# A four-mixer decoder layer: matmuls placed by a clock of two engines, norm sums in float32r, buffers of the closing parts

## The chip, the cores and the metric

The kernel runs on one core of one Trainium2 chip. A core has TensorE (matmuls, from SBUF into PSUM), VectorE, ScalarE and GpSimd, and SyncE, which here only issues DMAs. The metric is the device time in microseconds, the median of several runs.

## The reference

One layer of a hybrid decoder over a prompt of 1024 positions and, beside it, 8 single-position samples with states of their own. Both go through the same weights, so the kernel treats them as 1032 columns.

```python
hn = rmsnorm(x, norm_mix_g)
proj = hn @ w_in                       # 1024 -> 2836, columns shared out among four mixers
o_s5  = s5_mixer(...)                  # complex diagonal recurrence, gelu, gate
o_ssd = ssd_mixer(...)                 # conv, scan; rmsnorm over 256 channels of y * silu(z)
o_hg  = hgrn2_mixer(...)               # gated scan; rmsnorm over 64 channels of each head, gate
o_gla = gla_mixer(...)                 # gated scan; rmsnorm over 64 channels of each head, gate
x = x + concat(o_s5, o_ssd, o_hg, o_gla) @ w_out
hn = rmsnorm(x, norm_mlp_g)
x = x + square(relu(hn @ w_up)) @ w_down      # 1024 -> 4096 -> 1024
y = rmsnorm(x, norm_final_g)           # and the final states of the four mixers
```

All is float32.

## The kernel before

Activations lie transposed, channels on the 128 partitions and positions along the columns. The columns are cut in two halves, `hf` 0 with 512 and `hf` 1 with 520 (two chunks of 260, `CK`). A large product takes its two operands split by `split` into a high and a low float32r part (ScalarE copies `hi`, VectorE subtracts to get `lo`) and adds three matmuls for each pair (`mm3`): high with high, high with low, low with high. So one output tile of 128 rows from 8 tiles of input takes 24 matmuls of 512 columns, or 48 of 260.

`main` issues the large products in this order: input projection of half 0 (`xA`), of half 1 (`xB`), output projection of half 0 (`mixA`), its MLP, output projection of half 1 (`mixB`), its MLP (in which `fast_up` forms blocks of the up product from sums and differences of blocks, `TS`), and `close`. `side` and `side2` issue the mixers of half 0 and then of half 1 as strands: Python generators that yield where the next matmul needs work of other engines. Their small products are plain float32.

`drive` merges main and strands into one order. It keeps a clock `pe` of TensorE, which `mm` advances by a planned cost; `lat` collects the planned latency of ScalarE and VectorE instructions of a strand's step, and after the step the strand is due again at `pe + wait()`. While no strand is due, main goes on by one product step. The order is a priority: the framework's scheduler then lists each engine's instructions by priority as its own model finds them ready, so an order on an engine can differ from the order of issue. Instructions under `first()` (evictions of the large products) and the weight preparation `wprep` go ahead of the rest. Each engine and each DMA queue then works through its list in order.

The places that the change touches:

- `gated` (mixers HGRN2 and GLA) and `ssd` end with a norm: ScalarE squares the outputs into `osq` or `ysq`, TensorE multiplies them by a constant matrix (`bo64`, blocks of 1/64, or `o256`, all 1/256) held in the constants `CS`, which sums over channels and spreads the sum, and ScalarE takes `Ln` and `Exp`. Then the mixer's two tiles are split into the mixed columns (`mixed`, `mix_split`) that the output projection reads. The projection takes its eight input tiles in `MIX_ORDER`, those of `ssd` (2 and 3) last.
- `outproj` needs, for each of its 8 tiles, the weights, a load of the input `x` and a PSUM bank or two of the four called `pm`. It adds the product to `x`, splits the scaled sum into `h2`, squares it into `sq` and stores it as `xd`. The first half is finished meanwhile: in `outproj(1)`, `finish(n)` for n below 8 calls `residual` (load `xr`, scale and add to `Y`) and `sumsq` (square into another `sq`, add into `fsq`).
- `x`, both `sq`, `xr`, the evictions and some more take turns in one set of four buffers, tag `io`. The mixers' pool `mp` has 13 buffers of the same size, tag `b`; the mixers use them till their end, and the pool is closed behind `outproj(1)`. The pool `late` opens in its place.
- `close` makes the last down products of half 1 in two column chunks, `c` 1 and then 0: eight tiles, each added to `Y`, squared, summed up, scaled by the gain; then the sum over channels on TensorE, the reciprocal root (`rstd`: `Ln`, `Exp` and a correcting step on VectorE), four scalings of `Y` by it and four stores.

Of the kernel before, what the change touches and what calls it, by code (L numbers as in the profile page):

```python
# [9 lines left out]
F32 = mybir.dt.float32  # L10
# [11 lines left out]
WM = 520  # L22
# [23 lines left out]
def _layout(items):  # L46
    d, o = {}, 0
    for n, w in items:
# [6 lines left out]
                     ('dsk', 2), ('sng', 2), ('lbl', 2), ('hng', 2), ('bgk', 1), ('gng', 1), ('wgk', 128)])  # L55
PS5, NPS5 = _layout([('lre', 8), ('lim', 8), ('ldt', 8), ('bglu', 2), ('Bre', 128), ('Bim', 128), ('Cre', 128),
                     ('Cim', 128), ('sd', 128), ('dsel', 16), ('iota', 128), ('wglu', 512)])
CST, NCST = _layout([('ident', 128), ('tri', 128), ('mneg', 128), ('bo64', 128), ('o256', 128),
                     ('ones', 128), ('id32', 32), ('sel2', 2), ('sel4', 4)])


def host_consts():
    c = np.zeros((128, NCST), np.float32)

    def put(n, v):
        o, w = CST[n]
        c[:, o:o + w] = v
    i = np.arange(128)
    put('ident', np.eye(128))
    put('tri', i[:, None] <= i[None, :])  # L70
    put('mneg', np.where(i[:, None] <= i[None, :], 0.0, -1e30))
    put('bo64', (i[:, None] // 64 == i[None, :] // 64) / 64.0)
    put('o256', 1.0 / 256)
    put('ones', 1.0)
    put('id32', i[:, None] % 32 == np.arange(32)[None, :])
    put('sel2', i[:, None] // 64 == np.arange(2)[None, :])
    put('sel4', i[:, None] // 32 == np.arange(4)[None, :])
    m = np.zeros((128, 5, 16), np.int32)
    j = i % 32
    for l in range(5):  # L80
        h = 1 << l
        blk = np.arange(16) // h
        m[:, l] = (j[:, None] // (2 * h) == blk[None, :]) & (j[:, None] % (2 * h) < h)
    return c, m.reshape(128, 80)
# [26 lines left out]
class Kern:  # L111
    def __init__(self, tc, ctx, I, O):
        self.tc, self.nc, self.ctx, self.I, self.O = tc, tc.nc, ctx, I, O
        self.uid = 0
        self.pe = self.lat = self.dlat = 0.0

    def first(self):
# [4 lines left out]
        self.uid += 1  # L122
        return f"{s}_{self.uid}"

    def b(self, shape, name='t'):
        pool, tag, nb = self.here[:3]
        return pool.tile([128] + list(shape), F32, tag='b' + tag, name=self.n(name), bufs=nb)

    def q8(self, shape, name='t'):
        pool, tag = self.here[:2]  # L130
        return pool.tile([128] + list(shape), F32, tag='q' + tag, name=self.n(name), bufs=2)

    def sm(self, shape, tag, dt=F32, bufs=1):
        return self.smp.tile([128] + list(shape), dt, tag=tag, name=self.n(tag), bufs=bufs)
# [20 lines left out]

    def act(self, out, in_, f=AF.Copy, **k):
        self.lat += 250 + width(out) / 1.2
        return self.nc.scalar.activation(out, in_, f, **k)  # L158

    def dve(self, out):  # L160
        self.lat += 90 + width(out) / 0.96

    def tt(self, out, a, b_, op=OP.mult):
        self.dve(out)
# [21 lines left out]
    def mm(self, out, l, r, start=True, stop=True, token=None, **k):  # L186

        n, m = width(r), width(l)
        if l.dtype == F32R:
            self.pe += n / 2.4  # L190
        elif m > 64:
            self.pe += 426 if n < 128 else 1.7 * n
        else:
            self.pe += max(80, 1.05 * n) if m > 32 else max(34, 0.58 * n)
        i = self.nc.tensor.matmul(out, l, r, start=start, stop=stop, **k)  # L195
        if token:
            self.tc.stamp_issue_order_token(i.ins, token)
        return i
# [133 lines left out]
                    main_on = False  # L332

    def wait(self):
        return self.lat * 1.5 + self.dlat + 400

    def need(self, hf, *names):
        return lambda: self.done[hf].issuperset(names)
# [2 lines left out]
    def setup(self):  # L341
# [11 lines left out]
        with Prio(tc, -4000000):  # L353
# [5 lines left out]
        nc.vector.memset(self.epsb, EPS)  # L359
        self.mean = self.cpool.tile([128, 128], F32, name='mean')  # L360
        nc.vector.memset(self.mean, 1.0 / 1024)
        self.PJ = [{n: self.dp.tile([64, 1024] if n in ('u0', 'u1') else [128, w], F32, name=f'pj{n}{h}') for n in IN_ORDER}
                   for h, w in enumerate(HW)]
        self.XD = [[self.dp.tile([128, w], F32, name=f'xd{h}{n}') for n in range(8)] for h, w in enumerate(HW)]
# [512 lines left out]
    def gated(self, hf, nm, q, k, f, vn, Tp, H, sel, state, o_state, p_state, mixi, gn, gates):  # L877
# [78 lines left out]
        if hf:  # L956
# [21 lines left out]
            for t in range(Tp):  # L978
# [3 lines left out]
                for s in range(H):  # L982
                    h = t * H + s
                    self.act(o[h // 2][64 * (h % 2):64 * (h % 2) + 64, 512:520], po[64 * t:64 * t + 64, s * 8:s * 8 + 8])
        sq, rs = (self.q8([2, WM], n) for n in ('osq', 'ors'))
        for ot in range(2):
            last = self.act(sq[:, ot, :w], o[ot][:, :w], AF.Square)
        table = self.lnexp(last, 'natural_log')
        yield self.need(hf, *gates)
        for ot in range(2):  # L990
            for c0, c1 in CK[hf]:
                p = self.px()
                self.mm(p[:, :c1 - c0], self.cst('bo64'), sq[:, ot, c0:c1])
                self.after(self.act(rs[:, ot, c0:c1], p[:, :c1 - c0], AF.Ln, bias=self.epsb), table)
        self.act(rs[:, :, :w], rs[:, :, :w], AF.Exp, scale=-0.5)
        for ot in range(2):
# [190 lines left out]
    def ssd(self, hf):  # L1187
# [139 lines left out]
        for g_ in range(2):  # L1327
            z = self.get(hf, f'z{g_}') if hf else zs[g_]
            self.stt(y[g_][:, :w], X[g_][:, :w], self.prm('dsk')[:, g_:g_ + 1], y[g_][:, :w], OP.mult, OP.add)
            self.tt(y[g_][:, :w], y[g_][:, :w], z[:, :w])  # L1330
            q = self.b([WM], 'ysq')
            last = self.act(q[:, :w], y[g_][:, :w], AF.Square)
            sq.append(q)
        table = self.lnexp(last, 'natural_log')
        yield
        rs = self.b([WM], 'yrs')
        for c0, c1 in CK[hf]:
            p = self.px()
            for g_ in range(2):
                self.mm(p[:, :c1 - c0], self.cst('o256'), sq[g_][:, c0:c1], g_ == 0, g_ == 1)  # L1340
            self.rstd(rs[:, c0:c1], p[:, :c1 - c0], newton=False, table=table)
        for g_ in range(2):
            self.stt(y[g_][:, :w], y[g_][:, :w], self.prm('sng')[:, g_:g_ + 1], rs[:, :w], OP.mult, OP.mult)
            self.mixed(hf, 2 + g_, y[g_])


    def sumsq(self, hf, x, n, ssq):
        w = HW[hf]
        if n == 0:
            last = self.act(ssq[:, :w], x, AF.Square)  # L1350
        else:
            sq = self.sp.tile([128, WM], F32, tag='io', name=self.n('sq'), bufs=4)
            last = self.act(sq[:, :w], x, AF.Square)
            self.tt(ssq[:, :w], ssq[:, :w], sq[:, :w], OP.add)
        return last
# [33 lines left out]
    def residual(self, hf, Y, n, R):  # L1389

        w = HW[hf]
        x = self.sp.tile([128, WM], F32, tag='io', name=self.n('xr'), bufs=4)
        self.nc.sync.dma_start(x[:, :w], self.XD[hf][n])
        y = Y[:, n, :w]
        self.tt(y, y, R[:, :w])
        self.tt(y, y, x[:, :w], OP.add)
# [229 lines left out]
    def finish(self, i):  # L1626
# [2 lines left out]
        w = HW[0]  # L1629
        if i < 8:  # L1630
            self.residual(0, Y, i, R)
            self.last = self.sumsq(0, Y[:, i, :w], i, ssq)
        elif i == 8:
            self.final = Y, self.square_factors(0, ssq, self.last), ssq
        elif i > 8:
# [5 lines left out]
    def close(self, A, X2, ssq, first):  # L1641
# [3 lines left out]
        for c in (1, 0):  # L1645
            c0, c1 = CK[1][c]
            for n in range(8):
# [5 lines left out]
                x = X2[:, n, c0:c1]  # L1653
                sq = ssq[:, c0:c1] if n == 0 else self.sp.tile([128, WM], F32, tag='io', name=self.n('sq'), bufs=4)[:, c0:c1]
                with self.first():
                    self.tt(x, p, x, OP.add)
                    self.act(sq, x, AF.Square)
                    if 0 < n < 7:
                        self.tt(ssq[:, c0:c1], ssq[:, c0:c1], sq, OP.add)
                    self.act(x, x, AF.Copy, scale=self.prm('gf')[:, n:n + 1])  # L1660
# [3 lines left out]
            with self.first():  # L1664
                R = self.rows('R')[:, c0:c1]
                self.rstd(R, p)
                for n in range(0, 8, 2):
                    x = X2[:, n:n + 2, c0:c1]
                    self.tt(x, x, R[:, None].to_broadcast([128, 2, c1 - c0]))
                    nc.sync.dma_start(self.O['y'][n:n + 2, :, H0[1] + c0:H0[1] + c1].rearrange("n p c -> p n c"), x)  # L1670


# [195 lines left out]
```

## Time and profile before

| | us |
|---|---|
| median of 3 runs | 1239.98 (1239.54 to 1240.44) |
| the profiled execution | 1238.58 |
| its span, first to last instruction | 1236.8 |
| TensorE busy | 1203.4 (97%) |
| VectorE busy | 898.2 (73%) |
| ScalarE busy | 616.8 (50%) |
| GpSimd busy | 95.1 (8%) |

Busy time of TensorE is the union of its matmuls, whose ends are modelled, and matmuls overlap; so two records' distance in start, not the length of one, tells what a matmul costs in a row of them. An engine's idle time counts only where it holds up what ends last. The granted clock is a share of TensorE's full speed: 1.00 is 2.4 GHz, 0.50 is 1.2 GHz.

### The profile page before, as it was taken

How to read it: one execution, taken by the hardware profiler on the slowest of the kernel's cores; microseconds unless marked ns; L12 is line 12 of the kernel's file. 1: busy time of each engine (PE TensorE's matmuls, PEld its weight loads, DVE VectorE, ACT ScalarE, POOL GpSimd, SP SyncE). 2: the span in 40 equal slices, each digit the busy share in tenths (PEclk: the TensorE clock that was granted, in tenths of full speed). 3: DMA queues.
4: the chain of work that ended last, by engine and by line, in shares of the span. 5: the costliest groups of instructions: out<-in, count | busy, mean ns of one | idle time of the engine just before them, and what ended most of it. 6: DMA issues, size and time to landing. Idle time of an engine off the chain costs nothing. (4 is left out here: it accounts for less than half of the span.)

```text
span 1236.8 us, 23757 instructions
## 1 busy us (share of the span) xinstructions
PE 1203.4 (97%) x9107; PEld 1053.7 (85%) x9107; DVE 898.2 (73%) x1999; ACT 616.8 (50%) x1118; POOL 95.1 (8%) x155
## 2 busy tenths in 40 slices
PE   7999999999999999999999999999899999999996
PEld 5778888889978877787778787899799999999996
DVE  7998759876579559756666855577787766776895
ACT  7353362576344562535345732534675644654554
POOL 1113130000000100001000000001001100100100
PEclk9999999999999999999999999999899999999998
DMA  5564363355444442243224234346553332233332
GB/s 194 182 193 126 128 197 125 118 209 180 138 136 148 127 140 85 88 135 109 95 80 146 95 106 134 104 156 207 169 196 95 102 100 99 78 111 103 121 95 69
DMA packets 86048, 161.40 MB, mean 130 GB/s; under 512 B 13408, under 2 KB 19200, under 8 KB 85680
## 3 DMA queue, kind: packets, MB, share of 16 engines
q1 hardware_dynamic: 75952, 128.85, 33.2%
q0 software_dynamic: 9984, 31.05, 7.4%
q8 instruction: 71, 1.16, 0.4%
q14 instruction: 41, 0.34, 0.1%
HBM read 134.70 MB, written 25.16 MB: 129 GB/s over the span
## 5 line engine op out<-in xcount | busy, mean ns | idle before, releaser
L158 ACT ACTIVATE hi<-raw 128x512 fp32r<-128x512 f32 x362 | 223.5, 628 | 416.7 <-PE pm L195 315.8
L165 DVE TENSOR_TENSOR lo<-raw,hi 128x512 fp32r<-128x512 f32 x362 | 246.3, 684 | 103.3 <-ACT hi L158 94.9
L195 PE MATMUL pm<-a,hi 128*128 128x260 f32 (+1 forms) x1088 | 275.1, 340 | 1.9 <-DVE a L165 1.1
L195 PE MATMUL pm<-h,hi 128*128 128x512 f32 (+1 forms) x976 | 251.6, 347 | 5.7 <-DVE x L165 4.8
L195 PEld LDWEIGHTS pm<-a,hi 128*128 128x128 f32 x1088 | 183.8, 189 | 26.5 <-issue 2.4
L195 PEld LDWEIGHTS pm<-h,hi 128*128 128x128 f32 x976 | 167.5, 190 | 30.4 <-DVE x L165 5.0
L195 PE MATMUL pm<-a,lo 128*128 128x260 f32 (+1 forms) x544 | 172.2, 338 | 0.0
L195 PE MATMUL pm<-h,lo 128*128 128x512 f32 (+1 forms) x488 | 164.9, 345 | 0.0
L195 PE MATMUL pm<-xB,hi 128*128 128x260 f32 x704 | 118.8, 288 | 0.0
L195 PE MATMUL pm<-xA,hi 128*128 128x512 f32 x352 | 114.8, 406 | 1.0 <-ACT hi L158 1.0
L195 PEld LDWEIGHTS pm<-a,lo 128*128 128x128 f32 x544 | 98.1, 189 | 11.3 <-DVE lo L165 0.2
L165 DVE TENSOR_TENSOR Y<-pm,Y 128x260 f32<-128x260 f32 (+1 forms) x120 | 63.5, 546 | 57.7 <-PE pm L195 57.4
L195 PEld LDWEIGHTS pm<-xB,hi 128*128 128x128 f32 x704 | 97.4, 188 | 4.9 <-issue 3.3
L195 PEld LDWEIGHTS pm<-h,lo 128*128 128x128 f32 x488 | 91.4, 190 | 11.4 <-issue 0.2
L195 PE MATMUL px<-a,hi 128*128 128x260 f32 x448 | 83.9, 283 | 0.0
L195 PEld LDWEIGHTS pm<-xA,hi 128*128 128x128 f32 x352 | 65.8, 190 | 18.2 <-ACT hi L158 2.1
L195 PE MATMUL pm<-xB,lo 128*128 128x260 f32 x352 | 72.5, 286 | 0.0
L195 PE MATMUL pm<-xA,lo 128*128 128x512 f32 x176 | 71.2, 405 | 0.1
L195 PEld LDWEIGHTS px<-a,hi 128*128 128x128 f32 x448 | 67.1, 188 | 0.0
L165 DVE TENSOR_TENSOR a<-r,a 128x260 fp32r<-128x260 f32 (+1 forms) x96 | 48.7, 511 | 10.0 <-ACT a L158 9.2
L195 PEld LDWEIGHTS pm<-xB,lo 128*128 128x128 f32 x352 | 54.5, 188 | 0.7 <-issue 0.6
L195 PE MATMUL px<-a,lo 128*128 128x260 f32 x224 | 51.9, 282 | 0.0
(428 smaller groups left out, 1996.4 us busy)
## 6 DMA issues: line engine op xcount, KB each, us to landing
raw<-in_w_dn_dram SPq DMA_DIRECT2D x128, 256.0 KB, 2.7
raw<-in_w_in_dram SPq DMA_DIRECT2D x88, 256.0 KB, 2.9
raw<-in_w_up_dram SPq DMA_DIRECT2D x72, 256.0 KB, 2.9
raw<-in_w_up_dram POOLq DMA_DIRECT2D x56, 256.0 KB, 3.0
raw<-in_w_out_dram SPq DMA_DIRECT2D x32, 256.0 KB, 3.1
x<-in_xT_dram SPq DMA_DIRECT2D x16, 260.0 KB, 3.3
x<-in_xT_dram SPq DMA_DIRECT2D x16, 256.0 KB, 3.5
xd<-x POOLq DMA_DIRECT2D x8, 260.0 KB, 3.0
```

The lines of the kernel that those rows point to most:

```text
L158: return self.nc.scalar.activation(out, in_, f, **k)
L165: return self.nc.vector.tensor_tensor(out, a, b_, op)
L195: i = self.nc.tensor.matmul(out, l, r, start=start, stop=stop, **k)
```

## The change

Three things are changed.

- The planner: a float32r matmul of n columns counts 0.454 n ns instead of n/2.4; ScalarE and VectorE get a clock each (`free`), which every one of their instructions advances from the later of its own end and `pe`; and `wait` takes the larger of one and a half latencies and the time by which the later of the two clocks is ahead of `pe`.
- The norm sums of `gated` and `ssd`: the squares are split into two float32r parts, and two float32r matmuls take the place of one float32 matmul. The two constant matrices become float32r tiles filled by GpSimd and leave the constants that are loaded.
- The closing parts: `residual` and `sumsq` of half 0 take `xr` and `sq` from the mixers' 13 buffers; in `close`, the four scalings and stores of the first chunk (`c` 1) are issued behind the last addition of the second.

```diff
 def act(self, out, in_, f=AF.Copy, **k):
     self.lat += 250 + width(out) / 1.2
+    self.hold(0, 100 + width(out) / 1.2)
     return self.nc.scalar.activation(out, in_, f, **k)
+
+def hold(self, e, t):
+    self.free[e] = max(self.free[e], self.pe) + t

 def dve(self, out):
     self.lat += 90 + width(out) / 0.96
+    self.hold(1, 65 + width(out) / 0.96)
...
     if l.dtype == F32R:
-        self.pe += n / 2.4
+        self.pe += 0.454 * n
...
 def wait(self):
-    return self.lat * 1.5 + self.dlat + 400
+    return max(self.lat * 1.5, max(self.free) - self.pe) + self.dlat + 400
...
+        self.bo64, self.o256 = (self.cpool.tile([128, 128], F32R, name=n) for n in ('bo64', 'o256'))
+        nc.gpsimd.memset(self.o256.bitcast(F32), 1.0 / 256)
+        nc.gpsimd.memset(self.bo64.bitcast(F32), 0.0)
+        for i in (0, 64):
+            nc.gpsimd.memset(self.bo64[i:i + 64, i:i + 64].bitcast(F32), 1.0 / 64)
...
-        sq, rs = (self.q8([2, WM], n) for n in ('osq', 'ors'))
+        sq, rs = self.q8([4, WM], 'osq', F32R), self.q8([2, WM], 'ors')
         for ot in range(2):
-            last = self.act(sq[:, ot, :w], o[ot][:, :w], AF.Square)
+            last = self.act(rs[:, ot, :w], o[ot][:, :w], AF.Square)
+            self.split(sq[:, ot, :w], sq[:, 2 + ot, :w], rs[:, ot, :w])
...
-                self.mm(p[:, :c1 - c0], self.cst('bo64'), sq[:, ot, c0:c1])
+                for i in range(2):
+                    self.mm(p[:, :c1 - c0], self.bo64, sq[:, 2 * i + ot, c0:c1], i == 0, i == 1)
...
-            sq.append(q)
+            r = [self.b([WM], 'ysr', F32R)[:, :w] for _ in range(2)]
+            self.split(*r, q[:, :w])
+            sq += r
...
-            for g_ in range(2):
-                self.mm(p[:, :c1 - c0], self.cst('o256'), sq[g_][:, c0:c1], g_ == 0, g_ == 1)
+            for i, q in enumerate(sq):
+                self.mm(p[:, :c1 - c0], self.o256, q[:, c0:c1], i == 0, i == 3)
...
-    def sumsq(self, hf, x, n, ssq):
+    def sumsq(self, hf, x, n, ssq, sq=None):
...
-            sq = self.sp.tile([128, WM], F32, tag='io', name=self.n('sq'), bufs=4)
+            if sq is None:
+                sq = self.sp.tile([128, WM], F32, tag='io', name=self.n('sq'), bufs=4)
...
-        x = self.sp.tile([128, WM], F32, tag='io', name=self.n('xr'), bufs=4)
+        x = self.sp.tile([128, WM], F32, tag='io', name=self.n('xr'), bufs=4) if hf else \
+            self.mp.tile([128, WM], F32, tag='b', name=self.n('xr'), bufs=13)
...
-            self.last = self.sumsq(0, Y[:, i, :w], i, ssq)
+            self.last = self.sumsq(0, Y[:, i, :w], i, ssq, self.mp.tile([128, WM], F32, tag='b', name=self.n('sq'), bufs=13))
...
-                    self.tt(x, p, x, OP.add)
+                    last = self.tt(x, p, x, OP.add)
...
                 self.rstd(R, p)
+            if c:
+                R1, c2 = R, c1 - c0
+                continue
+            for c0, c1, R, wait in ((c2, c2 + c2, R1, last), (0, c2, R, None)):
                 for n in range(0, 8, 2):
                     x = X2[:, n:n + 2, c0:c1]
-                    self.tt(x, x, R[:, None].to_broadcast([128, 2, c1 - c0]))
+                    with self.first():
+                        i = self.tt(x, x, R[:, None].to_broadcast([128, 2, c1 - c0]))
+                    if wait:
+                        self.after(i, wait)
                     nc.sync.dma_start(...)
```

## Rows read from the trace of the kernel before

**Rows 1.** The page: the span, busy time by engine, and two groups of instructions.

```profile
span 1236.8 us, 23757 instructions
...
PE 1203.4 (97%) x9107; PEld 1053.7 (85%) x9107; DVE 898.2 (73%) x1999; ACT 616.8 (50%) x1118; POOL 95.1 (8%) x155
...
L158 ACT ACTIVATE hi<-raw 128x512 fp32r<-128x512 f32 x362 | 223.5, 628 | 416.7 <-PE pm L195 315.8
...
L165 DVE TENSOR_TENSOR lo<-raw,hi 128x512 fp32r<-128x512 f32 x362 | 246.3, 684 | 103.3 <-ACT hi L158 94.9
```

**Rows 2.** Windows: stretch, its length, busy us of each engine (instructions), granted clock.

```profile
180.00:240.00 60.00, 56.80 (x1023) 51.92 (x1022) 54.80 (x134) 25.86 (x43) 3.79 (x7) 1.00 0.34 112
...
450.00:480.00 30.00, 27.09 (x263) 20.14 (x263) 24.83 (x54) 15.57 (x27) 0.00 (x0) 0.94 0.27 90
...
660.00:720.00 60.00, 57.62 (x310) 45.41 (x307) 46.94 (x110) 41.16 (x65) 0.00 (x0) 1.00 0.41 132
...
840.00:930.00 90.00, 83.42 (x655) 81.07 (x654) 68.04 (x126) 56.12 (x119) 7.72 (x15) 0.96 0.56 184
```

**Rows 3.** TensorE's waits: who waited for whom, us in total, times, longest.

```profile
PE pm L195 <- DVE x L165: 4.8, 1, 4.8
...
PE lv L195 <- DVE D L165: 1.8, 1, 1.8
...
PE px L207 <- DMA hi<-pjhi: 1.5, 1, 1.5
```

**Rows 4.** Timeline of TensorE (start, us); tiles `osq`, `ysq` there (ns min/median/max).

```profile
252.58 1.88 PE L195 MATMUL px<-osq,CS 128*128 128x512 f32 x4
...
680.11 1.91 PE L195 MATMUL px<-osq,CS 128*128 128x260 f32 x8
...
L195 PE MATMUL px<-osq,CS x24: 380/383/592, 252.6 to 681.6; 128*128 128x260 f32 x16, 128*128 128x512 f32 x8
...
L195 PE MATMUL px<-ysq,CS x12: 380/382/593, 340.3 to 795.3; 128*128 128x260 f32 x8, 128*128 128x512 f32 x4
```

**Rows 5.** Timelines of SyncE, GpSimd, VectorE near 865 us; landing times of `x` loads.

```profile
863.22 0.33 SPq L1365 DMA_DIRECT2D x<-in_xT_dram  x1
...
861.98 2.13 POOL L1535 DMA_DIRECT2D raw<-in_w_up_dram  x4
...
870.61 0.76 DVE L165 TENSOR_TENSOR x<-pm,x 128x260 f32<-128x260 f32 x2 [4.76 <-DMA x<-in_xT_dram]
...
DMA to landing us min/median/max: 2.9/3.5/7.3
```

**Rows 6.** Timeline of TensorE, 860 to 872 us, and the window behind its stall.

```profile
861.78 0.64 PE L195 MATMUL pm<-h,hi 128*128 128x260 f32 x4
...
862.26 0.40 PE L195 MATMUL pm<-h,lo 128*128 128x260 f32 x2
...
871.09 0.80 PE L195 MATMUL pm<-h,hi 128*128 128x260 f32 x2 [4.81 <-DVE x L165]
...
871.00:876.00 5.00, 4.91 (x24) 4.91 (x25) 4.76 (x10) 1.89 (x3) 0.55 (x1) 0.54 0.17 64
```

**Rows 7.** Timelines of VectorE, ScalarE and the chain that ended last, past 1220 us.

```profile
1221.07 2.52 DVE L165 TENSOR_TENSOR Y<-Y,R 128x520 f32<-128x520 f32 x4
...
1225.49 0.42 ACT L158 ACTIVATE sq<-Y 128x260 f32<-128x260 f32 x1
...
1225.03 0.43 DVE Y L165
...
1226.38 1.16 PE px L195 x4
...
1228.53 0.44 DVE nw L165
```

**Rows 8.** Tile `mixA` on VectorE, and the window from its first product.

```profile
L165 DVE TENSOR_TENSOR mixA<-y,mixA x2: 680/682/683, 349.3 to 350.5; 128x512 fp32r<-128x512 f32 x2
...
331.00:353.60 22.60, 18.48 (x72) 13.35 (x73) 1.36 (x2) 1.25 (x2) 1.00 0.36 108
```

More of the change, by code (lines that the diff above doesn't have):

```diff
@@ L57 @@
                      ('Cim', 128), ('sd', 128), ('dsel', 16), ('iota', 128), ('wglu', 512)])
-CST, NCST = _layout([('ident', 128), ('tri', 128), ('mneg', 128), ('bo64', 128), ('o256', 128),
-                     ('ones', 128), ('id32', 32), ('sel2', 2), ('sel4', 4)])
+CST, NCST = _layout([('ident', 128), ('tri', 128), ('mneg', 128), ('ones', 128), ('id32', 32), ('sel2', 2), ('sel4', 4)])
 def host_consts():
@@ L71, in host_consts @@
     put('mneg', np.where(i[:, None] <= i[None, :], 0.0, -1e30))
-    put('bo64', (i[:, None] // 64 == i[None, :] // 64) / 64.0)
-    put('o256', 1.0 / 256)
     put('ones', 1.0)
@@ L114, in __init__ @@
         self.uid = 0
+        self.free = [0.0, 0.0]
         self.pe = self.lat = self.dlat = 0.0
@@ L123, in n, with b, q8 @@
         return f"{s}_{self.uid}"
-    def b(self, shape, name='t'):
+    def b(self, shape, name='t', dt=F32):
         pool, tag, nb = self.here[:3]
-        return pool.tile([128] + list(shape), F32, tag='b' + tag, name=self.n(name), bufs=nb)
-    def q8(self, shape, name='t'):
+        return pool.tile([128] + list(shape), dt, tag='b' + tag, name=self.n(name), bufs=nb)
+    def q8(self, shape, name='t', dt=F32):
         pool, tag = self.here[:2]
-        return pool.tile([128] + list(shape), F32, tag='q' + tag, name=self.n(name), bufs=2)
+        return pool.tile([128] + list(shape), dt, tag='q' + tag, name=self.n(name), bufs=2)
     def sm(self, shape, tag, dt=F32, bufs=1):
```

## The prediction

> **What bounds the kernel now.** I read the page's busy shares first. TensorE is busy for 1203.4 of 1236.8 us; no other engine passes 73% [rows 1]. So the end moves only by work taken off TensorE, by idle time of TensorE that goes away, or by the tail in which TensorE has finished. Next I cut the span into stretches and looked where TensorE's busy time falls short of the stretch [rows 2]. 180 to 240 us lacks 3.2 us and 450 to 480 lacks 2.9 (there the granted clock is 0.94 too); 660 to 720 lacks 2.4, and 840 to 930 lacks 6.6. The first three are where the mixers' matmuls are laid between the large products; the fourth is where the second half's output projection passes into its MLP. Then the list of TensorE's waits names who was late [rows 3]: VectorE's `D` (1.8 us), a load of `hi` (1.5), and, longest of all behind the start, VectorE's `x`, one wait of 4.8 us.
>
> I followed that one back. At 866 us the projection is over, and the MLP's second tile stands still until 871.09 for a PSUM bank, which frees when `x<-pm,x` has run [rows 6]. VectorE had idled 4.76 us in front of it, waiting for the load of `x` [rows 5]. SyncE issued this load only at 863.22, and the slowest load of `x` took 7.3 us against a median of 3.5, while GpSimd issued four weight loads from 861.98 [rows 5]. So late issue and traffic together made the stall. `x`, `sq` and, for the finished half, `xr` and another `sq` take turns in the four `io` buffers, so one tile of the projection uses up all four, and the next `x` must wait for the tile before it.
>
> **The change, part by part.**
>
> *Norm sums.* Before, each float32 matmul shows as two records. Four records of 512 columns stand 0.43 us apart ((1.88 - 0.59)/3, where 0.59 is one record alone), eight of 260 columns 0.22 apart ((1.91 - 0.38)/7) [rows 4]. So one matmul costs 0.86 or 0.44 us. `osq` has 24 records and `ysq` 12, which is 6 matmuls of 512 and 12 of 260 columns [rows 4]. After, each becomes two float32r matmuls. A float32r matmul of 260 columns takes 0.12 us, since two more of them lengthen a run from 0.40 to 0.64 [rows 6]; per column that makes 0.236 us for 512, an estimate from this row. Saved: 6 x (0.86 - 0.47) + 12 x (0.44 - 0.24) = 2.3 + 2.4 = 4.7 us of TensorE time. The Trainium skill (TensorE: Matmul & The Clock Gate, Back-to-back issue gap) gives about 216 ns for 512 columns at the full clock; by it the first bracket would be 0.43 and the part 0.2 us larger, and the row, which is longer, decides.
>
> It adds one ScalarE copy (0.63 us) and one VectorE subtraction (0.68) per squared tile, 12 of each [rows 1], so 7.6 and 8.2 us in all. They lie beside TensorE's products at 252 to 795 us; without that cover they would cost about 1.3 to 2 us in each of six chains. Nothing is queued behind them that the products need at once, since evictions go first in the order. Bounds: 0 (every saved microsecond turns into a wait for the mixers) to 4.7. I take 4.7, because TensorE is full where most of these matmuls lie.
> The two constant matrices come from four small GpSimd fills instead of a DMA; four of GpSimd's instructions would be some 2.5 us at its mean (95.1 us over 155 [rows 1]) if anything waited for them, but they are needed first at 252 us [rows 4], so I cost them at nothing.
>
> *Buffers of the closing part of the first half.* `xr` and `sq` of `finish` move to the mixers' pool of 13 buffers, which the mixers have left by then (their last `ysq` matmul starts at 795.3 [rows 4]). `io` then serves two tiles an iteration rather than four, and `x` can be asked for about one whole iteration, 5.8 us (48 matmuls of 0.12), earlier. The eight `xr` loads leave SyncE's queue without waiting for a buffer; the weights and `x` behind them on that queue can only gain. `x` of the last tile then lands around 861 with the usual 3.5 us, 4 to 5 us before TensorE needs the bank. So 4.8 us of stall go. After the stall the granted clock in 871 to 876 is 0.54: 92% of the 5 us at the lower level of 1.2 GHz, and work done at half speed in 4.6 us would take 2.3 [rows 6]. Full gain 7.1 us. What comes next: `TS`, whose loads follow the MLP's first block and shift with it, so its waits stay. The weight buffers of the later pool may lie where the 13 buffers lay and then start after `finish`'s last tile instead of at 862; they are first used behind the MLP's first block (384 matmuls of 0.12, some 46 us), which hides this. Bounds 0 (the load is late for its traffic alone) to 7.1; I take 6.5, as issue time is the larger part.
>
> *Closing part of the second half.* Four scalings `Y<-Y,R` of the first column block now sit on VectorE from 1221.07 for 2.52 us, in front of the last additions, and the closing sum starts only at 1226.38, behind a late `ssq` [rows 7]. Moved behind the last addition (1225.03 + 0.43), they leave `ssq` done by then; the sum then waits for the last `Y` and its square only (1225.49 + 0.42), so its last two records, 0.22 apart and 0.38 long, end at about 1226.55 instead of 1227.54. But now the four scalings occupy VectorE from 1225.46 to about 1227.95. The reciprocal root's VectorE steps began 0.99 behind the sum (1228.53); they would be ready at 1227.55 and may queue behind the scalings by 0.4 us. Their four stores move along, on SyncE's queue, where nothing else is left but the last four, and are issued before those. The added order waits on VectorE itself, and behind it stand only the root's steps and the last scalings. Gain 0.3 to 1.0, and 0.6 is taken.
>
> *The clock of ScalarE and VectorE.* `wait` grows where either engine's planned queue runs past the step's own latency, and never shrinks by this edit; at the same time a float32r column counts 0.454 instead of 0.417, so fewer products are laid into the same wait (8%). No instruction is added. What it can win is the idle time of the first three stretches, 3.2 + 2.9 + 2.4 = 8.5 us, and the slow clock in the second: 0.06 short of full in 30 us is 3.6 us at the lower level, 1.8 us lost [rows 2]. Together 10.3. VectorE is busy 54.8 of 60 us in the first stretch, so a queue that the old clock did not see is real there. But the load of `hi` is no queue of either engine, and a matmul placed later is one that delays its mixer. Bounds: a loss of 18 as in rival 3, to a gain of 10.3; I take a third of the gain, 3.5, since only part of the idle time stands behind a queue of VectorE.
>
> **Sum.** 4.7 + 6.5 + 0.6 + 3.5 = 15.3 us. The profiled execution took 1238.6 with a span of 1236.8, so it would be 1223.3; the runs' median, 1240.0, is 1.4 above the profiled one, so the median becomes 1224.7.
>
> **Rivals.**
> 1. *Handed back.* The norm sums and the placing free TensorE in the first half, but the mixers there are a chain of waits, and the projection cannot finish a tile without mixed columns 2 and 3. Their last split starts at 350.5 and takes 0.68 [rows 8]. TensorE has four banks, and six of eight columns ready, 72 matmuls; 72 had run by 353.6 [rows 8]. So about 2 us are to spare, and what the first half saves beyond that is lost. Without the first half's share (2.3, and 3.2/8.5 of the 3.5, 1.3) and half of the stall's gain (3.3) 8.4 us are left: 1232. For it: the slack is small. Against: 8% fewer products per wait also bring the chain forward.
> 2. *All of it.* Every mixer gap closes, 10.3 instead of 3.5: 22.1, so 1218. Against: one gap is a load's, and closing gaps in one place shifts steps everywhere.
> 3. *Slower, through the first half's chain alone.* The queue clock lengthens the waits of its three interleaved strands, the last split comes late by more than the 2 us to spare, and TensorE idles at the first projection. It decides from about 14 us of delay on (2 to spare and the 11.8 of the other parts), and 20 us gives 1246 (20 - 2 - 11.8 = 6.2 lost). The Trainium skill (TensorE: Matmul & The Clock Gate, HAM oscillation) says that a long idle stretch puts the array back to its lower clock; the trace agrees, with 0.54 behind the wait of 4.8 us. For it: VectorE is 91% busy at 180 to 240. Against: what is late there is late already, whichever order is written.
> 4. *No change.* The stall stays, since the load is late by traffic, and placing costs what the norm sums save: 1238 to 1242.
>
> **How the numbers follow.** Within 0.2% means 2.5 us here, about what repeated runs of this kernel can tell. Forecast, 1218 to 1231: 0.52. Handed back, 1231 to 1237: 0.18. All of it, 1214 to 1218: 0.10. No change: 0.07. Slower: 0.13. Faster is 0.80, same 0.07, slower 0.13. The likeliest is 1224.7; the range from 1214 to 1237 leaves out the last two.
>
> **What the profile after would show.** the norm sums with as many records as before (24 and 12), but 0.24 and 0.12 us apart; loads of `x` in the second projection issued before their product ends, no wait of TensorE there above 1 us, and a full granted clock behind it; `Y<-Y,R` in one run of eight near the end and the closing sum less than 1.5 us behind the last product; less idle time in the first three stretches. It is wrong if TensorE idles at the first projection, if `x` still lands late, or if new waits on the mixers come up elsewhere with a lower clock behind them.

## The result, and the profile after

The median went from 1239.8 to 1217.2 us (1216.4 to 1218.6), a ratio of 0.982 [0.980, 0.984]: 22.5 us, where 15.3 were forecast. The time lies inside the range, but below the band of the forecast itself (1218 to 1231) and in that of the rival "All of it" (1214 to 1218). The page of the profile after, its span and its busy times (against [rows 1]):

```profile
span 1214.6 us, 23758 instructions
...
PE 1192.8 (98%) x9107; PEld 1047.9 (86%) x9107; DVE 905.5 (75%) x2011; ACT 621.4 (51%) x1128; POOL 96.2 (8%) x159
```

The span is 22.2 us shorter. 10.6 of that is busy time of TensorE, 11.6 is time in which it idled (33.4 before, 21.8 now). The list of TensorE's waits after (who waited for whom, us in total, times, longest) no longer has the wait for `x` or the load of `hi` of [rows 3], and behind the start no wait above 1.7 us:

```profile
PE dl L199 <- DVE wdl L169: 6.1, 1, 6.1
PE lv L199 <- DVE R L174: 1.7, 1, 1.7
PE pm L199 <- ACT hi L157: 1.4, 3, 0.7
```

Windows after, for the stretches of [rows 2], the fourth moved forward with the projection, and one from the start to the first matmul of the second half's output projection, `mixB` (stretch, length, busy us of the engines, clock):

```profile
180.00:240.00 60.00, 59.18 (x1055) 54.70 (x1055) 53.36 (x132) 25.12 (x41) 4.12 (x8) 1.00 0.38 121
450.00:480.00 30.00, 28.31 (x423) 22.05 (x422) 27.48 (x59) 9.28 (x18) 0.00 (x0) 1.00 0.23 73
660.00:720.00 60.00, 60.00 (x296) 46.97 (x295) 43.64 (x88) 32.55 (x52) 0.00 (x0) 1.00 0.34 107
820.00:910.00 90.00, 89.95 (x739) 88.75 (x739) 68.62 (x131) 58.26 (x123) 8.59 (x16) 1.00 0.58 187
...
0.00:803.30 803.30, 791.97 (x5805) 650.96 (x5806) 595.86 (x1383) 394.71 (x651) 61.96 (x95) 1.00 0.44 138
```

The same last window of the kernel before:

```profile
0.00:815.00 815.00, 799.55 (x5805) 654.37 (x5806) 586.83 (x1370) 389.34 (x639) 60.83 (x91) 1.00 0.43 135
```

This window is the yardstick for all that follows: both hold 5805 matmuls, the whole first half and all mixers. It is 11.7 us shorter, 7.6 of it busy time and 4.1 idle time. The projection `mixB` takes as long as before. From the MLP of the second half to the last matmul's start it was 366.3 us (860.8 to 1227.1) and is 355.8 (849.0 to 1204.8): 10.5 less. Behind the last matmul, which is one of the closing sum, nothing is won.

Timeline of TensorE after (start, us, instructions; idle time in brackets), against [rows 4], [rows 6] and [rows 7]:

```profile
251.60 1.09 PE L199 MATMUL px<-osq,bo 128*128 128x512 f32 x4
252.53 0.63 PE L199 MATMUL pm<-xB,hi 128*128 128x260 f32 x4
...
665.74 0.64 PE L199 MATMUL px<-osq,bo 128*128 128x260 f32 x4
666.22 0.40 PE L199 MATMUL pm<-h,lo 128*128 128x512 f32 x1
...
848.73 0.40 PE L199 MATMUL pm<-mixB,lo 128*128 128x260 f32 x2
848.97 0.64 PE L199 MATMUL pm<-h,hi 128*128 128x260 f32 x4
...
1203.54 0.70 PE L199 MATMUL px<-ssq,mean 128*128 128x260 f32 x2
1204.51 0.71 PE L199 MATMUL px<-sq,mean 128*128 128x260 f32 x2 [0.27 <-ACT sq L157]
```

Four norm records of 512 columns now take 0.93 us from their start to the next product's. Two float32r matmuls, of one record each, stand in the place of one float32 matmul, so what took 0.86 now takes 0.47; four of 260 take 0.48, so 0.24 instead of 0.44. These are the forecast's two sizes. The MLP follows the projection without a gap. The closing sum starts as the last product ends.

Timeline of VectorE at the end after, against [rows 7]:

```profile
1203.58 0.43 DVE L169 TENSOR_TENSOR Y<-pm,Y 128x260 f32<-128x260 f32 x1
1203.92 2.52 DVE L169 TENSOR_TENSOR Y<-Y,R 128x520 f32<-128x520 f32 x4
1206.36 0.42 DVE L169 TENSOR_TENSOR nw<-R 128x260 f32<-128x260 f32 x1
...
1208.08 2.53 DVE L169 TENSOR_TENSOR Y<-Y,R 128x520 f32<-128x520 f32 x4
```

The sum ends at 1205.22 (1204.51 + 0.71), and the root's first step on VectorE starts 1.14 us later, when the scalings leave VectorE; before, 0.99 later. The forecast's sign of one run of eight `Y<-Y,R` did not come: they stand in two runs of four, with the root's steps between.

### The profile page after: what moved, and what is told of

The parts are those of the page before. It is cut to its first block, busy times and chain, and to the rows that moved or that the text cites. A ratio compares the mean times of both kernels' runs of the same rounds, so it can differ in the third digit from the quotient of the medians.

```text
span 1214.6 us, 23758 instructions
## 1 busy us (share of the span) xinstructions
PE 1192.8 (98%) x9107; PEld 1047.9 (86%) x9107; DVE 905.5 (75%) x2011; ACT 621.4 (51%) x1128; POOL 96.2 (8%) x159
## 5 line engine op out<-in xcount | busy, mean ns | idle before, releaser
L199 PE MATMUL pm<-h,hi 128*128 128x512 f32 (+1 forms) x976 | 246.9, 344 | 0.2 <-DVE u L169 0.2
L199 PEld LDWEIGHTS pm<-h,hi 128*128 128x128 f32 x976 | 164.7, 188 | 24.3 <-issue 2.0
L199 PE MATMUL pm<-h,lo 128*128 128x512 f32 (+1 forms) x488 | 162.0, 343 | 0.0
L199 PEld LDWEIGHTS pm<-a,lo 128*128 128x128 f32 x544 | 97.6, 188 | 11.3 <-issue 0.3
L199 PEld LDWEIGHTS pm<-h,lo 128*128 128x128 f32 x488 | 89.6, 188 | 11.4 <-issue 0.5
L199 PEld LDWEIGHTS pm<-xA,hi 128*128 128x128 f32 x352 | 66.0, 190 | 20.1 <-ACT hi L157 3.9
L1551 POOL DMA_DIRECT2D raw<-in_w_up_dram x56 | 30.0, 538 | 283.6 <-DVE lo L169 176.4
```

What stands on the lines that cost most here:

```text
L1551: self.nc.gpsimd.dma_start(x, self.I['w_up'][fb * 4 + 2 * pr + f][:, 512 * c:512 * c + 512])
```

## The experiments

Each ratio is to the kernel before, timed on the same chip, with its 95% interval; the us are the ratio times that kernel's median there. The window "to `mixB`" is the one above, from one profile of each kernel. Three kernels are alike up to its end and show how well it repeats: the kernel before (815.0), buffers alone (816.7) and `close` alone (814.5). So its length repeats within 2.2 us, TensorE's busy time within 2.8 and its idle time within 1.5. Up to the last matmul of the first output projection the same three repeat within 0.5 us (385.9, 385.5, 386.0).

| kernel | ratio | us | to `mixB` | TensorE busy, idle in it |
|---|---|---|---|---|
| before | 1 | 0 | 815.0 | 799.6, 15.4 |
| the change | 0.982 [0.980, 0.984] | -22.5 | 803.3 | 792.0, 11.3 |
| buffers alone | 0.9930 [0.9914, 0.9946] | -8.7 | 816.7 | 800.4, 16.3 |
| norm sums alone | 0.9993 [0.9978, 1.0007] | -0.9 | 816.8 | 798.8, 18.0 |
| planner alone | 0.9903 [0.9882, 0.9924] | -12.0 | 805.5 | 794.5, 11.0 |
| `close` alone | 0.9995 [0.9984, 1.0007] | -0.6 | 814.5 | 797.6, 16.9 |
| the change without norm sums | 0.9827 [0.9806, 0.9848] | -21.4 | 806.7 | 795.4, 11.3 |
| the change without the two clocks | 0.9805 [0.9786, 0.9823] | -24.1 | 803.6 | 791.9, 11.7 |
| the change without the column cost | 0.9987 [0.9976, 0.9998] | -1.6 | 823.4 | 801.6, 21.8 |
| the change, fills later | 0.9809 [0.9791, 0.9827] | -23.7 | 802.0 | 791.3, 10.7 |
| column cost alone | 0.9963 [0.9950, 0.9977] | -4.6 | 811.3 | 797.5, 13.8 |
| two clocks alone | 1.0008 [0.9996, 1.0021] | +1.0 | 816.9 | 800.0, 16.9 |
| no clocks, fills later | 0.9806 [0.9790, 0.9823] | -24.0 | 802.5 | 791.1, 11.4 |
| the same with a cost of 0.5 | 0.9873 [0.9855, 0.9891] | -15.7 | 809.8 | 796.6, 13.2 |

### Buffers alone

```diff
...
-        x = self.sp.tile([128, WM], F32, tag='io', name=self.n('xr'), bufs=4)
+        x = self.sp.tile([128, WM], F32, tag='io', name=self.n('xr'), bufs=4) if hf else \
+            self.mp.tile([128, WM], F32, tag='b', name=self.n('xr'), bufs=13)
...
-            self.last = self.sumsq(0, Y[:, i, :w], i, ssq)
+            self.last = self.sumsq(0, Y[:, i, :w], i, ssq, self.mp.tile([128, WM], F32, tag='b', name=self.n('sq'), bufs=13))
```

> Only the move of xr and sq of the first half's finish to the mixers' pool, all else as before. Theory A (the four io buffers made the load of x late): the stall of 4.8 us at 866 and the slow clock behind it go, and with them the TS waits of 1.1 us some 55 us later; 7 to 9 us faster, and no other stage moves. Theory B (the whole change's new order of instructions removed the stall): less than 3 us faster, the stall stays.

Timeline of SyncE, then of VectorE, then two windows: the stall's stretch, and the MLP and close of the second half:

```profile
855.54 0.42 SPq L1366 DMA_DIRECT2D x<-in_xT_dram  x1
```

```profile
862.41 0.77 DVE L165 TENSOR_TENSOR x<-pm,x 128x260 f32<-128x260 f32 x2 [1.57 <-PE pm L195]
```

```profile
862.00:878.00 16.00, 16.00 (x131) 15.52 (x130) 13.59 (x24) 12.02 (x27) 2.13 (x4) 1.00 0.49 166
...
862.30:1219.40 357.10, 354.58 (x2919) 351.39 (x2918) 272.11 (x562) 201.81 (x439) 28.37 (x53) 1.00 0.35 112
```

The same two windows of the kernel before:

```profile
862.00:878.00 16.00, 11.19 (x76) 10.98 (x75) 9.62 (x17) 5.27 (x10) 3.72 (x7) 0.79 0.57 193
...
860.80:1227.10 366.30, 357.64 (x2918) 353.64 (x2918) 277.54 (x570) 205.91 (x444) 31.03 (x58) 0.99 0.35 113
```

The last `x` is asked for at 855.54, some 6.8 us before the projection's end at 862.33; before, at 863.22, 2.4 us behind it. VectorE now waits for the product and not for the load. In 862 to 878 TensorE runs 131 matmuls at the full clock; the kernel before ran 76 there, at 0.79. Over MLP and close 9.2 us are won, 6.1 idle and 3.1 busy. The idle part is more than the stall: the three waits for `r` and `TS` behind it (0.51, 0.34, 0.73 us) are gone too. Theory A has it: one edit, and the stall, its slow clock and the waits behind it go together.

### Norm sums alone

Only the hunks of `host_consts`, `b`, `q8`, the four fills, `gated` and `ssd`:

```diff
-                self.mm(p[:, :c1 - c0], self.cst('bo64'), sq[:, ot, c0:c1])
+                for i in range(2):
+                    self.mm(p[:, :c1 - c0], self.bo64, sq[:, 2 * i + ot, c0:c1], i == 0, i == 1)
...
-            for g_ in range(2):
-                self.mm(p[:, :c1 - c0], self.cst('o256'), sq[g_][:, c0:c1], g_ == 0, g_ == 1)
+            for i, q in enumerate(sq):
+                self.mm(p[:, :c1 - c0], self.o256, q[:, c0:c1], i == 0, i == 3)
```

> Only the norm sums in two float32r matmuls with the two constant matrices filled by GpSimd. Theory A (TensorE is full, so its work counts): 4.7 us faster, 2.3 of it by the end of the input projections. Theory B (the mixers of the first half are a chain that gives saved work back): the first output projection starts where it did, and 1 to 2.5 us are left.

Timeline of TensorE, four of its waits:

```profile
26.87 0.74 PE L192 MATMUL pm<-xA,hi 128*128 128x512 f32 x2 [0.77 <-ACT hi L155]
39.20 0.70 PE L192 MATMUL pm<-xA,hi 128*128 128x512 f32 x2 [0.64 <-DVE ev L162]
...
685.13 0.96 PE L192 MATMUL pm<-a,hi 128*128 128x512 f32 x3 [1.28 <-ACT hi L155]
693.75 0.66 PE L204 MATMUL px<-CS,xa 128*128 128x128 f32 x4 [2.68 <-ACT ors L155]
```

The sums got shorter, but the window to `mixB` did not: its 816.8 us and its busy time lie within what repeats, its idle time 1.1 us above. Its stages tell more. The last matmul of the first half's input projection starts at 158.3 us (156.2 before), that of the second half's at 331.8 (331.8), that of the first output projection at 388.8 (385.9). So the first stage loses 2.1 us (the waits at 26.87 and 39.20 lie in it), the second wins them back, and the output projection loses 2.9. Its last mixed column is split at 358.3 instead of 350.5 [rows 8]:

```profile
L162 DVE TENSOR_TENSOR mixA<-y,mixA x2: 628/652/677, 356.7 to 358.3; 128x512 fp32r<-128x512 f32 x2
```

That is Theory B's chain: the first output projection starts where it did. Whether the added split, the longer planned waits or another order made the chain late was not separated. What the whole kernel gains lies behind the window, where the stall is 2.5 us instead of 4.8 in this profile; over the whole no difference can be measured, and Theory A's 4.7 us lie outside the interval.

Taken out of the whole change instead (the diff is against the change, and takes back the fills, splits and constants with it), the sums with their fills are worth 3.4 us to `mixB` by two profiles, and 1.1 by the two savings, whose intervals overlap.

```diff
-                for i in range(2):
-                    self.mm(p[:, :c1 - c0], self.bo64, sq[:, 2 * i + ot, c0:c1], i == 0, i == 1)
+                self.mm(p[:, :c1 - c0], self.cst('bo64'), sq[:, ot, c0:c1])
...
-            for i, q in enumerate(sq):
-                self.mm(p[:, :c1 - c0], self.o256, q[:, c0:c1], i == 0, i == 3)
+            for g_ in range(2):
+                self.mm(p[:, :c1 - c0], self.cst('o256'), sq[g_][:, c0:c1], g_ == 0, g_ == 1)
```

> The whole change without its norm sums: planner, buffers and close stay. Theory A (the norm sums save 4.7 us once the planner has taken the mixers' waits away): 17.5 to 18.5 us faster than before instead of 22.5. Theory B (what the norm sums save is waited away, and their fills and new order cost some 2 us in the first stage): 21 to 24 us faster, as much as the whole change.

The time is Theory B's, but only half of its reason holds. Without sums and fills the first half's input projection ends 2.0 us earlier (156.0 instead of 158.0); behind it the sums save 5.4 us to `mixB`. With the fills listed later (below) the window is 802.0 instead of 806.7, which is the forecast's 4.7, to the 2.2 us that the window repeats; 2.9 of it are there by the end of the first output projection (384.8 to 381.9). The ratios, 0.9827 and 0.9809, can't tell this.

### `close` alone

```diff
-                    self.tt(x, p, x, OP.add)
+                    last = self.tt(x, p, x, OP.add)
...
+            if c:
+                R1, c2 = R, c1 - c0
+                continue
+            for c0, c1, R, wait in ((c2, c2 + c2, R1, last), (0, c2, R, None)):
...
```

> Only the close: the first chunk's scalings and stores behind the last addition. Theory A (as predicted): the closing sum starts about 1 us earlier behind the last product and the end comes 0.6 us earlier. Theory B (the scalings take back on VectorE what the sum gains): within 0.2 us of before.

Timeline of TensorE, the closing sum, in the kernel before and then with this edit:

```profile
1226.38 0.71 PE L195 MATMUL px<-ssq,mean 128*128 128x260 f32 x2 [1.39 <-DVE ssq L165]
```

```profile
1222.30 0.71 PE L195 MATMUL px<-ssq,mean 128*128 128x260 f32 x2
1223.27 0.71 PE L195 MATMUL px<-sq,mean 128*128 128x260 f32 x2 [0.26 <-ACT sq L158]
```

The wait of 1.39 us for `ssq` in front of the sum is now 0.26 for `sq`; behind the sum's end 9.6 us follow (1223.98 to 1233.6) instead of 9.3. The ratio can't tell the two theories apart.

### The planner alone, and taken apart

First the whole of it on the kernel before:

```diff
+        self.hold(0, 100 + width(out) / 1.2)
...
+        self.hold(1, 65 + width(out) / 0.96)
...
-            self.pe += n / 2.4
+            self.pe += 0.454 * n
...
-        return self.lat * 1.5 + self.dlat + 400
+        return max(self.lat * 1.5, max(self.free) - self.pe) + self.dlat + 400
```

> Only the planner: 0.454 ns a float32r column, the clocks of ScalarE and VectorE, and the larger of two in wait. Theory A (each part adds to the others): what the other parts leave of 22.5 us, so 7 to 9 us faster, in the MLP of the first half and between 180 and 240 us. Theory B (the placing moves waits about and pays only together with the other parts): within 2.5 us of before.

Windows, a stretch of mixers in the MLP and the one to `mixB`:

```profile
450.00:480.00 30.00, 30.00 (x403) 23.25 (x402) 26.62 (x52) 9.00 (x16) 0.00 (x0) 1.00 0.26 82
...
0.00:805.50 805.50, 794.50 (x5805) 653.38 (x5806) 588.87 (x1370) 394.11 (x641) 60.92 (x91) 1.00 0.43 137
```

450 to 480, which lacked 2.9 us and ran at 0.94, is full at full clock. To `mixB` 9.5 us are won, 4.4 idle and 5.1 busy. The stall of the second projection stays (a wait for `x` of 4.1 us), as the buffers are the old ones. So placing is worth about three times the 3.5 us that the forecast gave it, and more than either theory gave: 12.0 us [9.4, 14.6]. The next four kernels ask which of its two halves does that: in the whole change, without the engine clocks; in the whole change, without the column cost; and each half alone on the kernel before. The change without the clocks (diff against the change):

```diff
-        self.hold(0, 100 + width(out) / 1.2)
...
-        self.hold(1, 65 + width(out) / 0.96)
...
-    return max(self.lat * 1.5, max(self.free) - self.pe) + self.dlat + 400
+    return self.lat * 1.5 + self.dlat + 400
```

> The whole change without the clocks of ScalarE and VectorE: the column cost of 0.454, the norm sums, buffers and close stay, wait is as before. Theory A (the clocks place the matmuls): the waits between 450 and 720 us come back, 11 to 14 us faster than before. Theory B (the column cost does it): 20 us faster or more.

Nothing that can be measured is lost: 0.9805 [0.9786, 0.9823] beside 0.982 [0.980, 0.984], and the same busy and idle time to `mixB`.

The change without the column cost (diff against the change):

```diff
-            self.pe += 0.454 * n
+            self.pe += n / 2.4
```

> The whole change without the column cost: the clocks of ScalarE and VectorE, norm sums, buffers and close stay, a float32r column counts 1/2.4 ns. Theory A (the clocks place the matmuls): 19 us faster or more, few waits between 450 and 720 us. Theory B (the column cost does it): 11 to 14 us faster, the waits there come back.

Nearly all of the change is lost, more than Theory B gave. Timeline of TensorE at the first output projection, and the window around it:

```profile
350.38 0.49 PE L199 MATMUL px<-ysr,o 128*128 128x512 f32 x1 [0.32 <-DVE ysr L169]
354.48 0.70 PE L199 MATMUL px<-U,G 128*128 128x136 f32 x4 [3.60 <-DMA U<-pjs]
...
357.90 1.28 PE L199 MATMUL px<-U,G 128*128 128x136 f32 x4 [1.89 <-ACT yrs L157]
361.30 1.22 PE L199 MATMUL pm<-mixA,hi 128*128 128x512 f32 x2 [2.11 <-ACT mixA L157]
```

```profile
326.00:396.00 70.00, 62.08 (x306) 49.20 (x305) 51.77 (x138) 30.56 (x52) 4.57 (x10) 0.93 0.39 125
```

The change itself there:

```profile
326.00:390.00 64.00, 64.00 (x328) 53.98 (x327) 48.61 (x107) 32.51 (x55) 5.29 (x12) 1.00 0.54 166
```

The products of the input projection run out at 325.4 instead of 331.8, so fewer are left to lie under the first half's mixers. Then TensorE stands three times for the mixers' last steps, 7.6 us in all (3.60 for a load of `U`, 1.89 for `yrs`, 2.11 for `mixA`), and the granted clock is 0.93 over the stretch. This is rival 3 in its place and kind. In the change itself 326 to 390 is busy throughout, and the last matmul of `mixA` starts at 382.8; here it starts at 394.9. These 12.1 us are part of the 20.1 that are lost to `mixB`; the other 8.0 go in the first half's MLP, where 4.4 us of idle time stand between 690 and 707.

The column cost alone (diff against the kernel before):

```diff
-            self.pe += n / 2.4
+            self.pe += 0.454 * n
```

> Only the column cost, 0.454 instead of 1/2.4 ns; wait has no clocks, all else as before. Theory A (a clock of TensorE that ran 8% slow put every mixer step too late, and its cost alone is the gain of the placing): 8 to 12 us faster, as the run with cost and clocks together. Theory B (cost and clocks are both needed): less than 5 us faster.

Timeline of TensorE, the two largest new waits:

```profile
649.16 0.73 PE L195 MATMUL pm<-a,hi 128*128 128x512 f32 x2 [2.17 <-ACT hi L158]
651.11 1.11 PE L207 MATMUL px<-CS,xa 128*128 128x128 f32 x4 [1.21 <-ACT xa L158]
```

The column cost alone brings 4.6 us of the 12.0, as in Theory B. To `mixB` it is 5.8 us behind the planner alone, 5.0 of them in the first half's MLP. There new waits of 4.8 us in all come up at 642 to 652, and the granted clock is 0.83 in 640 to 660. Why they come up without the clocks was not followed.

The two clocks alone (diff against the kernel before):

```diff
+        self.hold(0, 100 + width(out) / 1.2)
...
+        self.hold(1, 65 + width(out) / 0.96)
...
-    return self.lat * 1.5 + self.dlat + 400
+    return max(self.lat * 1.5, max(self.free) - self.pe) + self.dlat + 400
```

> Only the clocks of ScalarE and VectorE with the larger of two in wait; a column counts 1/2.4 ns as before. Theory A (the clocks only delay mixers, and the first half's chain has about 2 us to spare): TensorE idles at the first output projection, 5 to 12 us slower. Theory B (they place the matmuls better): 3 us faster or more.

The clocks alone change nothing that can be measured; neither theory's number came. Theory A's place did. The input projection again ends at 325.4, and TensorE again waits at the first output projection:

```profile
352.78 0.73 PE L202 MATMUL px<-U,G 128*128 128x136 f32 x4 [1.36 <-ACT yrs L160]
356.17 2.15 PE L202 MATMUL pm<-mixA,hi 128*128 128x512 f32 x5 [2.66 <-ACT mixA L160]
```

The kernel before, with 0.417 and no clocks, has no wait there, and the change, with both, has none either. So it takes the clocks with the low cost to make these waits.

So the halves don't add. On the kernel before: cost -4.6, clocks +1.0, both -12.0. On the other three parts: cost alone -24.1, clocks alone -1.6, both -22.5. In one set the clocks help the cost by some 7 us, in the other no help can be measured. The other three parts without any of the planner were not run, so what the planner is worth on top of them is not measured.

### The fills, and the cost once more

The four fills listed behind GpSimd's others, once in the change and once in the change without the two clocks:

```diff
-        nc.gpsimd.memset(self.o256.bitcast(F32), 1.0 / 256)
-        nc.gpsimd.memset(self.bo64.bitcast(F32), 0.0)
...
+        with Prio(tc, 500000):
+            nc.gpsimd.memset(self.o256.bitcast(F32), 1.0 / 256)
+            nc.gpsimd.memset(self.bo64.bitcast(F32), 0.0)
...
```

> The whole change with its four GpSimd fills behind the three large ones of the S5 setup instead of ahead of them. Theory A (a VectorE instruction at the start lasts until GpSimd's fill ends, so each fill ahead delays the first products): TensorE's first matmul starts at 5.8 us as before instead of 6.1, and the whole is 0.3 to 2 us faster than the whole change. Theory B (the fills are hidden): as the whole change, 22.5 us faster than before.

> The whole change without the clocks of ScalarE and VectorE and with its four fills behind the large ones. Theory A (the clocks are worth nothing, the fills' place some 1.5 us): 24.5 to 26 us faster than before, the fastest of all. Theory B (the two gains do not add): 22 to 24 us.

There the constants cost the first stage nothing. In the change with later fills the first matmul stays at 6.10 us (5.81 before, 6.09 in the change), but the waits at 15.5, 26.3 and 38.8 us are gone, and the last matmul of the first half's input projection starts at 155.8 instead of 158.0 (before: 156.2). Without the clocks too it starts at 155.4 instead of 157.7, and here the first matmul comes at 5.81, as Theory A of the first said; the last section shows that such a difference comes between traces of the same start. Over the whole kernel the intervals hold all four theories' numbers: 0.9809 and 0.9806 can't be told from each other, from 0.9805 without the clocks or from the change's 0.982. What orders the three waits was not settled.

The second of these with a cost of 0.5:

```diff
-            self.pe += 0.454 * n
+            self.pe += 0.5 * n
```

> As the run without the clocks and with late fills, but a column counts 0.5 ns, more than it takes (120 ns for 260 columns is 0.46). Theory A (the true cost is what places best): 2 us or more slower than that run, with more waits of TensorE on the mixers. Theory B (the earlier the better, whatever is true): 2 us or more faster than that run.

Window to `mixB`, and the records of `ssd`'s norm sums (ns min/median/max, first to last start):

```profile
0.00:809.80 809.80, 796.55 (x5806) 652.33 (x5807) 595.46 (x1383) 396.30 (x653) 61.21 (x95) 1.00 0.43 137
```

```profile
L192 PE MATMUL px<-ysr,o x12: 278/282/393, 313.2 to 717.9; 128*128 128x260 f32 x8, 128*128 128x512 f32 x4
```

A cost above the true one loses 8.3 us against 0.454: Theory A's time, but not its waits on the mixers. A float32r column takes 0.46 ns by [rows 6] (0.12 us for 260), so the value nearest to the row is the best of the three tried (with 0.417 there is the change without the column cost, which keeps the clocks, and, without clocks, the kernel before against the column cost alone). Each cost also gives another order of all instructions, and three values can't tell a rule from a lucky order. The last norm sum starts at 717.9, some 44 us earlier than with 0.454 (761.5), which wins nothing, as the second projection comes behind the first half's MLP anyway. Of the 7.3 us lost to `mixB` only 1.9 is idle time; 5.4 is busy time at an equal clock, spread over many small groups. What makes those longer stays open.

## Why the prediction was right, and where its sizes were wrong

**Norm sums, 4.7.** The step from rows to TensorE time held: 0.47 and 0.24 us instead of 0.86 and 0.44. Two steps failed. One is "so I cost them at nothing", of the fills: ahead of the other fills they cost the first stage about 2 us (158.0 instead of 156.0 or 155.8), and behind them nothing. The other is "I take 4.7, because TensorE is full where most of these matmuls lie": alone the sums bring 0.9 us [-0.9, 2.7], as the first half's last mixed column comes 7.8 us later and the first output projection loses 2.9. That is the first rival's mechanism, for this part and on the old planner. In the whole change that column is split at 346.1, ahead of the 350.5 before, and the sums save 1 to 3 us with their fills; without the fills' cost the traces show the 4.7, to some 2 us.

**Buffers, 6.5.** Right in place and cause: early loads, no stall, full clock, no wait above 1 us. Mis-sized: 9.2 us in the trace and 8.7 in the ratio. The step "so its waits stay" failed: those for `r` and `TS` went with the stall (idle 6.1, not 4.8), and the busy time fell by 3.1, not 2.3.

**Closing part, 0.6.** The sum ends 1.68 us behind the last product's end instead of 2.54, and the root's VectorE steps start 0.15 later behind it (up to 0.4 was allowed for), so 0.7 net. The ratio alone, 0.9995 [0.9984, 1.0007], can't tell this from nothing.

**Placing, 3.5.** Right in sign and too small by more than half: 8.3 us to `mixB` (815.0 to 806.7, the change without norm sums) to 9.5 (the planner alone), and 12.0 in the ratio. The step that failed is "I take a third of the gain, since only part of the idle time stands behind a queue of VectorE". In the whole change the queues were not the point: the column cost, which the forecast named only as "8% fewer products per wait", does the work, and the engine clocks do nothing measurable. On the old kernel cost and clocks were both needed, and why only there is open. Half of the gain is also busy time, 5.1 us of the planner alone, where like kernels differ by up to 2.8; the forecast counted no busy time beyond 1.8 us of slow clock.

**Rivals.** "All of it" has the number, but not by its mechanism: the mixers' idle time did not all go (450 to 480 still lacks 1.7 us), and the buffers brought 2.7 us more than forecast. That its 22.1 us meet the measured 22.5 is luck. "Handed back" is what the norm sums alone show. "Slower" was real as a mechanism: with the clocks in the planner it appears as soon as the column cost is put back, and the one number 0.454 keeps it off. The single parts add to 22.2 us (8.7 + 0.9 + 12.0 + 0.6), close to 22.5; since the planner's halves don't add, that is no proof that the parts do.

## What to carry to other kernels

A planner that lays small work between large products needs the large products' cost: read it from the distance of their starts in the trace. Here the value nearest to the row, 0.46 ns a column, was the best of three: 0.417 with the engine clocks left TensorE waiting for the last mixers at the projection that needs them, and 0.5 lost 8.3 us. On another kernel try values on both sides. Time taken off the busiest engine counts only where nothing else is late next, so test it alone and in company before adding it up. A wait for a load is best followed back to the buffer that let the load be issued; the fix here was two lines.

## What the runs showed of the hardware

A VectorE instruction over four columns lasted until a GpSimd fill ended. Timelines of GpSimd and VectorE in the change with later fills:

```profile
2.48 1.80 POOL L637 MEMSET Q<- 128x2048 f32 x1
4.22 0.95 POOL L713 MEMSET TT<- 128x1024 f32 x1
```

```profile
2.84 2.36 DVE L175 TENSOR_SCALAR ae<-PR 128x4 f32<-128x4 f32 x1
```

VectorE without the clocks and with later fills, whose `Q` and `TT` start at the same 2.48 and 4.22:

```profile
2.85 1.46 DVE L168 TENSOR_SCALAR ae<-PR 128x4 f32<-128x4 f32 x1
```

The first ends at 5.20, 0.03 behind the fill of `TT` (5.17), the second at 4.31, 0.03 behind that of `Q` (4.28). In the kernel before it lasts 1.42 us and ends at 4.31 behind `Q`'s fill (4.28), in the change 1.75 and 4.60 behind `Q`'s (4.57). Others of that form, of four columns too, take 0.17 us. Which of the two fills it is changes between traces of the same start: of the seven kernels without the new fills four show `Q`'s and a first matmul at 5.80 or 5.81, three show `TT`'s and 5.99. `wdl` and the first matmul queue behind it. So the fills ahead, which nobody waits for, moved the start by some 0.28 us in either case (6.09 behind `Q`'s in three traces, 6.28 behind `TT`'s in one; with later fills 5.81 in two and 6.10 in one), and a single trace's 0.2 us there says nothing of an edit. The Trainium skill (SBUF — State Buffer, Who interferes with whom) says that a VectorE `tensor_scalar` can need the port pair that it shares with GpSimd, and that whichever comes second is blocked until the other's instruction is over; the rows agree that the wait lasts to a fill's end. That a fill whose record starts at 4.22 goes ahead of an instruction that starts at 2.84 does not fit "whichever comes second", and there the rows decide.

The clock can also fall without a long stall. In the kernel before, 64 matmuls of two columns (466.94 to 467.81) are followed by one large matmul and a wait:

```profile
469.43 0.80 PE L195 MATMUL pm<-a,hi 128*128 128x512 f32 x1 [1.11 <-DVE a L165]
```

The granted clock is 1.00 in 466 to 468, 0.50 (the level of 1.2 GHz) in 470 to 472 and 1.00 again in 474 to 476. Longer waits of the same trace left it at 1.00: 1.83 us in front of 196.54 (196 to 206), 1.54 in front of 458.85 (458 to 466), 1.30 in front of 702.04 (700 to 712). So the length of a wait alone does not tell here. The Trainium skill (TensorE: Matmul & The Clock Gate, A second HAM failure mode: psum-queue depth-cycling) says that frequent short idle times between groups of matmuls can move the clock down and up; the trace shows two, of 0.18 us in front of the 64 matmuls and of 1.11 us behind them, and agrees in that no long one was needed.
